# Gate products of 256 columns, issued through the helper of the large sums

## The chip, the cores and the metric

The kernel runs on one core of one Trainium2 chip. The metric is device time in microseconds of one launch. The profile comes from one execution and tells the span from the first to the last instruction; the device time of that execution is a little longer than its span.

## The reference, cut to what matters

One layer of a block with three parallel branches over 256 latent tokens and 256 context tokens of width 2048. The two places that the change touches are the recurrent gates (a block-diagonal product per head, two directions, two gates) and the pooling products (one 256 x 256 matrix per group):

```python
def _block_diag(u, w, b):                       # 8 heads of 128 channels
    y = jnp.einsum("blhi,hij->blhj", uh, w) + b
...
def _lru_coeffs(u, wr, br, wi, bi, lam):
    r = jax.nn.sigmoid(_block_diag(u, wr, br))
    i = jax.nn.sigmoid(_block_diag(u, wi, bi))
    log_a = -LRU_C * r * jax.nn.softplus(-lam)
    return jnp.exp(log_a), jnp.sqrt(-jnp.expm1(2.0 * log_a)) * i * u
...
def _multiscale_pool(u, n_rows, w_pool, s_pool):  # 4 groups of 256 channels
    ...                                           # p: window mean minus the token itself
    y = jnp.einsum("brngi,gij->brngj", p, w_pool)
    return y.reshape(bs, L, W_B) * s_pool
```

Around them stand an input projection of 2048 to 13312 columns, a depthwise convolution ahead of the recurrence and another of 31 taps, a layer norm, output projections of the branches, merge gates and a last projection.

## The kernel before, in words

Every fp32 product is made of three fp32r matmuls. Each operand is split into a high part (a cast by ScalarE) and a low part (a subtraction by VectorE), and high x high, high x low and low x high are summed in one PSUM bank.

**The large sums.** A weight piece of 128 x 2048 lands in `raws`, is split into `wh` and `wl` (line 84 and the helper at line 210), and is the stationary operand; the activations, `hH` and `hL`, 16 slots of 512 columns each, are the moving one. Most sums have 256 columns (the latent tokens) and 16 blocks of the contraction. The helper `columns` (lines 258 to 269) issues for each block high x high and high x low (lines 265, 266), and behind all of these the 16 low x high products (line 269): 48 matmuls of 256 columns.

**The short product.** `recent["pe"]` notes whether the last matmuls were wide (512 columns) or "columns" (256). Where a sum of 256 columns begins behind wide ones, `lead_in` (lines 250 to 256) issues one product of 64 columns first, on line 255; its result is overwritten by the sum. `wide` (line 245) issues one dummy product of 512 columns on line 247; one stands behind the pooling product, the layer norm's sums and the gate's sums.

**The recurrent gates.** Once the first projection is done (about 150 us), the context columns of `hH` and `hL` (256 to 512 of each slot) are free and serve as slots for smaller operands: the convolved input `u` of two heads in slots 8 to 11, the gate weights of one head in slots 14 and 15. `products(h, d)` (line 619) makes both gates of a head for one direction, over 512 tokens: per gate one bank of the small pool and three matmuls of 512 columns by `mm3` (lines 238 to 241). It is called 16 times. `gates` then reads the two banks with ScalarE (line 634 on).

**The pooling products.** `pool_end(g)` (line 846) is called once for each of the 4 groups. It makes two halves of a bank; each half sums two blocks of the contraction, by `mm3` on 256 columns. Its weights lie in slots 6 and 7, its input in slots 12 and 13. A wide dummy product follows.

**What sets the order.** The steps of the large sums are a fixed list. At each step the weights of the next one are split, work that has come due is issued (the pooling products among it), then the step's sum, and then as much background work as VectorE's estimated load leaves room for: the recurrence with its calls of `products` is such a chain. All 16 calls fall between large sums. Much later, at line 979, the output gate is summed with a matmul that waits for a chain of VectorE on weights which GpSimd's queue loads.

Of the kernel before, what the change touches and what calls it, by code (L numbers as in the profile page):

```python
# [145 lines left out]
def hybrid_block_kernel(  # L146
# [46 lines left out]
    def bank(pool=accp, tag="acc"):  # L193
        counter[0] += 1
        return pool.tile([P, 512], F32, tag=tag, name=f"{tag}{counter[0]}")

    def small_bank():
        return bank(smp, "sm")
# [9 lines left out]
    def tt(o, a, b, op):  # L208
        load["V"] += 0.09 + 0.00104 * size(o)
        V.tensor_tensor(out=o, in0=a, in1=b, op=op)  # L210
# [8 lines left out]
    def stt(o, a, s, b, op0, op1):  # L219
        load["V"] += 0.13 + 0.00104 * size(o)  # L220
        V.scalar_tensor_tensor(o, a, s, b, op0=op0, op1=op1)  # L221
# [5 lines left out]
    def scan(o, a, b, init):  # L227
        load["V"] += 0.13 + 0.00104 * size(o)
        V.tensor_tensor_scan(o, a, b, initial=init, op0=ALU.mult, op1=ALU.add)
# [4 lines left out]
    def split(H, Lo, src):  # L234
        A.copy(H, src)  # L235
        tt(Lo, src, H.bitcast(F32), ALU.subtract)

    def mm3(ps, sh, sl, mh, ml, start, stop):
        T.matmul(ps, sh, mh, start=start, stop=False)  # L239
        T.matmul(ps, sh, ml, start=False, stop=False)  # L240
        T.matmul(ps, sl, mh, start=False, stop=stop)  # L241

    recent = {"pe": "wide"}

    def wide(ps):

        T.matmul(ps, hH[:, 2, 0:128], hH[:, 0:2, 0:256], start=True, stop=True)
        recent["pe"] = "wide"

    def lead_in(job):  # L250


        ps, wh, _, mh, _ = job
        if recent["pe"] == "wide" and ps.shape[-1] == 256:
            T.matmul(ps[:, 0:64], wh[0], mh[0][:, 0:64], start=True, stop=True)
        recent["pe"] = "wide" if ps.shape[-1] == 512 else "columns"

    def columns(jobs):

        lead_in(jobs[0])
        for ps, wh, wl, mh, ml in jobs:
            for k in range(len(wh)):
                T.matmul(ps, wh[k], mh[k], start=k == 0, stop=False)  # L265
                T.matmul(ps, wh[k], ml[k], start=False, stop=False)  # L266
        for ps, wh, wl, mh, ml in jobs:
            for k in range(len(wh)):
                T.matmul(ps, wl[k], mh[k], start=False, stop=k == len(wh) - 1)  # L269
# [101 lines left out]
    with tc.manual_schedule():  # L371
# [82 lines left out]
        for n, (a, b) in enumerate(x_parts):  # L454
# [5 lines left out]
            for k in range(a, b):  # L460
                for j in range(4):
                    w = o + 512 * k + P * j
# [72 lines left out]
        def slots(i, n):  # L535
            return cH[:, i:i + n, :], cL[:, i:i + n, :]
# [4 lines left out]
        def take(name, lst):  # L541
            r = lst[rot[name] % len(lst)]
            rot[name] += 1
            return r
# [62 lines left out]
        def lru():  # L607
            la, lt, li = [ar[:, o:o + 2048].rearrange("p (h d l) -> p h d l", h=2, d=2) for o in (A_LA, A_LT, A_LI)]
            uH, uL = slots(8, 4)
            wH, wL = slots(14, 2)  # L610
            pss = {}

            def weights(h):
                raw = ws_t[0]
                split(wH, wL, raw.rearrange("p (a b) -> p a b", a=2))
                if h < 7:
                    nc.gpsimd.dma_start(raw, w_lru[h + 1])

            def products(h, d):
                i = h % 2  # L620
                for g in range(2):
                    ps = small_bank()
                    w = slice(128 * g, 128 * (g + 1))
                    mm3(ps.rearrange("p (s l) -> p s l", s=2), wH[:, d, w], wL[:, d, w],
                        uH[:, 2 * i:2 * i + 2, :], uL[:, 2 * i:2 * i + 2, :], True, True)
                    pss[g] = ps
                recent["pe"] = "wide"
                if d == 1:
                    lru_at["mm"] += 1

            def gates(h, d):
                i, c = h % 2, 8 * d + h
                ad, td, idd = la[:, i, d, :], lt[:, i, d, :], li[:, i, d, :]
                A.activation(ad, pss[0], AF.Tanh, scale=0.5, bias=brh[:, c:c + 1])
                A.activation(idd, pss[1], AF.Tanh, scale=0.5, bias=bih[:, c:c + 1])
                A.activation(td, ad, AF.Tanh, scale=tsp[:, c:c + 1], bias=tsp[:, c:c + 1])
                A.activation(ad, ad, AF.Exp, scale=nsp[:, c:c + 1], bias=nsp[:, c:c + 1])

            def gated(h, d):
                i = h % 2  # L640
                stt(li[:, i, d, :], li[:, i, d, :], 1.0, u_t[h % 4], ALU.add, ALU.mult)

            weights(0)
            ahead = False
            for pr in range(4):
                h0, h1 = 2 * pr, 2 * pr + 1
                if not ahead:
                    yield lambda: lru_at["split"] > pr
                    yield "S"
                    products(h0, 0)  # L650
                    yield "S"
                gates(h0, 0)
                products(h0, 1)
                yield "S"
                gates(h0, 1)
                weights(h1)
                gated(h0, 0)
                yield "S"
                products(h1, 0)
                gated(h0, 1)  # L660
                yield "S"
                gates(h1, 0)
                products(h1, 1)
                yield "S"
                gates(h1, 1)
                if pr < 3:
                    weights(h1 + 1)
                gated(h1, 0)
                yield "S"
                A.activation(lt, lt, AF.Sqrt, scale=0.25)  # L670
                gated(h1, 1)
                lru_at["u"] += 1
                yield "S"
                for i in range(2):
                    stt(lt[:, i], la[:, i], 1.0, lt[:, i], ALU.add, ALU.mult)
                    yield
                for i in range(2):
                    tt(lt[:, i], lt[:, i], li[:, i], ALU.mult)
                    yield
                ahead = pr < 3 and lru_at["split"] > pr + 1  # L680
                if ahead:
                    products(h1 + 1, 0)
                    yield "S"
                for i in range(2):
                    f, b = li[:, i, 0, :], li[:, i, 1, :]
                    scan(f[:, 256:512], la[:, i, 0, 256:512], lt[:, i, 0, 256:512], 0.0)
                    scan(b[:, ::-1], la[:, i, 1, ::-1], lt[:, i, 1, ::-1], 0.0)
                    yield
                    scan(f[:, 0:256], la[:, i, 0, 0:256], lt[:, i, 0, 0:256], f[:, 511:512])
                    yield  # L690
                for i in range(2):
                    tt(ya[:, h0 + i, :], li[:, i, 0, 0:256], li[:, i, 1, 0:256], ALU.add)
                    yield
# [148 lines left out]
        def put_p(k, t, src):  # L842
            H, Lo = slots(pslot[k] + t, 1)
            first.append((step_no[0] + 1, lambda: split(H[:, 0, :], Lo[:, 0, :], src)))

        def pool_end(g):
            bg.need(f"pool{g}")
            pH, pL = slots(12, 2)
            wH, wL = slots(6, 2)
            ps = bank()  # L850
            for j in range(2):
                for k in range(2):
                    mm3(ps[:, 256 * j:256 * (j + 1)], wH[:, k, 128 * j:128 * (j + 1)],
                        wL[:, k, 128 * j:128 * (j + 1)], pH[:, k, :], pL[:, k, :], k == 0, k == 1)
            wide(bank())
            for j in range(2):
                t = 2 * g + j
                pf = take("pf", pf_t)
                stt(pf, ps[:, 256 * j:256 * (j + 1)], vt[:, V_PS + t:V_PS + t + 1], zz_t[j], ALU.mult, ALU.mult)
                put_p(1, t, pf)  # L860
# [185 lines left out]
        for kind, key, item, q in steps:  # L1046
# [16 lines left out]
            if kind in ("xa", "xb", "zb", "cv", "cg", "za", "zc"):  # L1063
                ps = bank()
# [4 lines left out]
            elif kind == "gl":  # L1069
# [5 lines left out]
                ps = state["gl"][:, 256 * q:256 * (q + 1)]  # L1075
# [5 lines left out]
            elif kind == "bout":  # L1081
                k, j = key
                state["bout"] = bank()
                H, Lo = slots(pslot[k], 8)
                jobs = []
# [9 lines left out]
            elif kind == "out":  # L1095
                recent["gate"] = True
                if q == 0:
# [5 lines left out]
                    if key == 3:  # L1103
                        ps = bank()
# [37 lines left out]
            elif kind == "pwc":  # L1142
# [4 lines left out]
                jobs = []  # L1147
                for j in range(2):
                    ct = 2 * key + j
                    ps = bank()  # L1150
# [80 lines left out]
```

## Time and profile before

| | us |
|---|---|
| runs, not profiled | 971.37, 972.97, 977.41 (median 972.97) |
| profiled execution, device time | 973.01 |
| its span, first to last instruction | 971.2 |
| TensorE busy in it | 947.6 (98%) |
| VectorE, ScalarE, GpSimd busy in it | 738.9, 497.3, 40.8 |

In the profile PE is TensorE with its matmuls, PEld its weight loads, DVE VectorE, ACT ScalarE, POOL GpSimd; a `q` behind one of them means its queue of instructions. A matmul's duration includes the time in which the next one already streams, so the pace of TensorE is read from the start times of successive matmuls.

### The profile page before, as it was taken

The page shows a single profiled execution, that of the slowest core. Times are in us where ns is not written, and L with a number is a line of the kernel's source. Part 1 is how long each engine was busy: PE and PEld are TensorE (multiplying, and loading weights), DVE is VectorE, ACT ScalarE, POOL GpSimd, SP SyncE. Part 2 cuts the span into 40 slices and gives each one's busy share as a digit, 9 for nine tenths or more (in the row PEclk, how much of TensorE's full clock was granted, in tenths as well). Part 3 has the DMA queues.
Part 4 walks back from the last instruction along what each step waited for, and adds up shares of the span by engine and source line. Part 5 has one row for each costly group of instructions (what it writes and reads, how often), then busy time and mean ns, then how long its engine had stood idle before and what let it go on. Part 6 is the DMA issues. An engine that isn't in the chain of part 4 may idle for free.

```text
span 971.2 us, 18386 instructions
## 1 busy us (share of the span) xinstructions
PE 947.6 (98%) x7675; PEld 881.5 (91%) x7675; DVE 738.9 (76%) x1134; ACT 497.3 (51%) x657; POOL 40.8 (4%) x74
## 2 busy tenths in 40 slices
PE   6899999999999999999999999999999999999996
PEld 3576679999999999999999999999999899998885
DVE  3445457867875876899999999996665887898864
ACT  3223336567666677674444534344674444444442
POOL 0000010000100000000000000000002011101000
PEclk9999999999999999999999999999999999999999
DMA  9799955555545554555555555555459788878542
GB/s 371 300 420 379 358 195 191 185 192 177 189 145 192 174 204 161 174 178 197 194 206 182 196 195 197 194 191 200 173 197 361 243 313 327 306 262 309 202 169 88
DMA packets 34724, 220.72 MB, mean 227 GB/s; under 512 B 4128, under 2 KB 4272, under 8 KB 11856
## 3 DMA queue, kind: packets, MB, share of 16 engines
q1 hardware_dynamic: 28080, 195.28, 55.6%
q0 software_dynamic: 6560, 24.26, 7.4%
q8 instruction: 60, 0.98, 0.4%
q14 instruction: 24, 0.20, 0.1%
HBM read 217.43 MB, written 2.10 MB: 226 GB/s over the span
## 4 chain that ended last, share of the span: by engine, by line
PE 95%; DMA 2%; DVE 1%; ACT 1%; issue 1%; SPq 0%; ACTq 0%; DVEq 0%
PE acc L265 24%; PE acc L266 24%; PE acc L269 24%; PE acc L504 7%; PE sm L409 3%; PE acc L1117 3%; PE acc L1119 3%; PE acc L1120 3%; DMA raws<-in_w_ada_dram 2%; PE sm L504 1%; PE sm L240 1%; PE sm L239 1%; PE sm L241 1%; ACT hH L433 0%; DVE ar L210 0%
## 5 line engine op out<-in xcount | busy, mean ns | idle before, releaser
L265 PE MATMUL acc<-hH,wh 128*128 128x256 f32 (+1 forms) x2000 | 466.8, 278 | 0.0
L266 PE MATMUL acc<-hL,wh 128*128 128x256 f32 (+1 forms) x2000 | 464.6, 277 | 0.0
L84 ACT CAST wh<-raws 128x1024 fp32r<-128x1024 f32 (+1 forms) x288 | 298.4, 1052 | 259.4 <-PE acc L266 220.1
L210 DVE TENSOR_TENSOR wl<-raws,wh 128x1024 fp32r<-128x1024 f32 (+1 forms) x288 | 339.4, 1217 | 107.3 <-ACT wh L84 53.7
L265 PEld LDWEIGHTS acc<-hH,wh 128*128 128x128 f32 x2000 | 375.6, 188 | 1.7
L266 PEld LDWEIGHTS acc<-hL,wh 128*128 128x128 f32 x2000 | 375.8, 188 | 0.7
L269 PE MATMUL acc<-hH,wl 128*128 128x256 f32 (+1 forms) x2000 | 253.4, 277 | 0.0
L269 PEld LDWEIGHTS acc<-hH,wl 128*128 128x128 f32 x2000 | 239.4, 188 | 0.7
L221 DVE SCALAR_TENSOR_TENSOR ar<-ar,vt 128x256 f32<-128x256 f32 (+1 forms) x264 | 115.3, 503 | 0.0
L210 DVE TENSOR_TENSOR ar<-ar 128x512 f32<-128x512 f32 (+8 forms) x126 | 79.5, 654 | 8.4 <-DMA ar<-in_xt_dram 7.0
L221 DVE SCALAR_TENSOR_TENSOR ar<-ar,sc 128x512 f32<-128x512 f32 x64 | 48.0, 751 | 18.3 <-DMA ar<-in_w_gate_dram 16.9
L1119 PE MATMUL acc<-wh,hH 128*128 128x512 f32 (+1 forms) x144 | 51.8, 369 | 0.0
L1120 PE MATMUL acc<-wh,hL 128*128 128x512 f32 (+1 forms) x144 | 51.3, 366 | 0.0
L210 DVE TENSOR_TENSOR hL<-ar,hH 128x256 fp32r<-128x256 f32 (+1 forms) x76 | 39.5, 548 | 12.3 <-ACT hH L235 11.7
L215 DVE TENSOR_SCALAR sml<-sm,vt 128x2 f32<-128x2 f32 x16 | 3.5, 219 | 45.0 <-PE sm L417 45.0
L504 PE MATMUL acc<-hH,wh 128*128 128x512 f32 x96 | 29.3, 415 | 4.7 <-ACT hH L433 3.4
L433 ACT ACTIVATE hH<-ar,sml 128x256 fp32r<-128x256 f32 x32 | 17.5, 595 | 31.0 <-DVE sml L215 31.0
L411 ACT COPY ar<-sm 128x256 f32<-128x256 f32 x16 | 6.0, 374 | 51.5 <-PE sm L409 51.5
L1117 PE MATMUL acc<-wl,hH 128*128 128x512 f32 (+1 forms) x144 | 32.1, 366 | 0.0
L1120 PEld LDWEIGHTS acc<-wh,hL 128*128 128x128 f32 x144 | 27.0, 188 | 4.8 <-issue 0.2
L1119 PEld LDWEIGHTS acc<-wh,hH 128*128 128x128 f32 x144 | 27.0, 188 | 4.8 <-issue 0.2
L221 DVE SCALAR_TENSOR_TENSOR ar<-ar,acc 128x256 f32<-128x256 f32 (+1 forms) x56 | 29.6, 529 | 0.7 <-ACT ar L918 0.4
(145 smaller groups left out, 697.5 us busy)
## 6 DMA issues: line engine op xcount, KB each, us to landing
raws<-in_w_br_dram SPq DMA_DIRECT2D x49, 1024.0 KB, 4.9
raws<-in_w_gl_dram SPq DMA_DIRECT2D x48, 1024.0 KB, 4.9
raws<-in_w_bout_dram SPq DMA_DIRECT2D x24, 1024.0 KB, 4.9
raws<-in_w_ada_dram SPq DMA_DIRECT2D x16, 1024.0 KB, 9.9
ar<-in_w_ada_dram SPq DMA_DIRECT2D x16, 1024.0 KB, 9.9
ar<-in_w_gate_dram POOLq DMA_DIRECT2D x32, 512.0 KB, 5.9
raws<-in_w_out_dram SPq DMA_DIRECT2D x16, 1024.0 KB, 4.9
ar<-in_w_xa_dram SPq DMA_DIRECT2D x5, 896.0 KB, 11.5
```

Of the source, the lines that this page charges most:

```text
L84: self.nc.scalar.copy(h[:, 0:w], src)
L210: V.tensor_tensor(out=o, in0=a, in1=b, op=op)
L221: V.scalar_tensor_tensor(o, a, s, b, op0=op0, op1=op1)
L265: T.matmul(ps, wh[k], mh[k], start=k == 0, stop=False)
L266: T.matmul(ps, wh[k], ml[k], start=False, stop=False)
L269: T.matmul(ps, wl[k], mh[k], start=False, stop=k == len(wh) - 1)
L409: T.matmul(ps[32 * j:32 * j + 32, :], sc[:, k, :], raw[:, q, :], start=k < 4, stop=k >= 12)
L433: A.activation(hH[:, kt, w], h[:, w], AF.Identity, scale=gg[:, s:s + 1], bias=sh[:, s:s + 1])
L504: T.matmul(xa_ps[t], (wh, wh, wl)[a][:, P * t:P * (t + 1)], (hH, hL, hH)[a][:, kt, :], start=kt == 0 and a == 0, stop=kt == KT - 1 and a == 2)
L1117: T.matmul(ps, H, wl[:, w], start=False, stop=kt == KT - 1)
L1119: T.matmul(ps, H, wh[:, w], start=kt == 0, stop=False)
L1120: T.matmul(ps, Lo, wh[:, w], start=False, stop=False)
```

## The change

`products` issues each gate as two halves of 256 columns (latent and context tokens), each half as one call of `columns` with a single block; `recent["pe"]` is then "columns" and no longer "wide". `pool_end` issues each half of its bank by `columns` with two blocks. `mm3` is not called any more.

```diff
             def products(h, d):
                 i = h % 2
+                jobs = []
                 for g in range(2):
                     ps = small_bank()
                     w = slice(128 * g, 128 * (g + 1))
-                    mm3(ps.rearrange("p (s l) -> p s l", s=2), wH[:, d, w], wL[:, d, w],
-                        uH[:, 2 * i:2 * i + 2, :], uL[:, 2 * i:2 * i + 2, :], True, True)
+                    jobs += [(ps[:, 256 * s:256 * (s + 1)], [wH[:, d, w]], [wL[:, d, w]], [uH[:, 2 * i + s, :]],
+                              [uL[:, 2 * i + s, :]]) for s in range(2)]
                     pss[g] = ps
-                recent["pe"] = "wide"
+                for job in jobs:
+                    columns([job])
...
             for j in range(2):
-                for k in range(2):
-                    mm3(ps[:, 256 * j:256 * (j + 1)], wH[:, k, 128 * j:128 * (j + 1)],
-                        wL[:, k, 128 * j:128 * (j + 1)], pH[:, k, :], pL[:, k, :], k == 0, k == 1)
+                columns([(ps[:, 256 * j:256 * (j + 1)], [wH[:, k, 128 * j:128 * (j + 1)] for k in range(2)],
+                          [wL[:, k, 128 * j:128 * (j + 1)] for k in range(2)], [pH[:, k, :] for k in range(2)],
+                          [pL[:, k, :] for k in range(2)])])
             wide(bank())
```

## Rows read from the trace of the kernel before

**Rows 1.** The page: span, engines, and the chain that ended last.

```profile
span 971.2 us, 18386 instructions
...
PE 947.6 (98%) x7675; PEld 881.5 (91%) x7675; DVE 738.9 (76%) x1134; ACT 497.3 (51%) x657; POOL 40.8 (4%) x74
...
PE 95%; DMA 2%; DVE 1%; ACT 1%; issue 1%; SPq 0%; ACTq 0%; DVEq 0%
```

**Rows 2.** Waits of TensorE: for whom, us in total, times, longest.

```profile
PE acc L446 <- DMA ar<-in_xt_dram: 6.9, 1, 6.9
...
PE acc L979 <- issue: 1.8, 1, 1.8
```

**Rows 3.** Groups of matmuls by line and shape: count, busy us, mean ns, idle before.

```profile
L265 PE MATMUL acc<-hH,wh 128*128 128x256 f32 x1984 | 460.4, 277 | 0.0
...
L239 PE MATMUL sm<-hH 128*128 128x512 f32 x32 | 12.6, 395 | 0.0
...
L255 PE MATMUL acc<-hH,wh 128*128 128x64 f32 x24 | 4.6, 192 | 0.0
...
L239 PE MATMUL acc<-hH 128*128 128x256 f32 x16 | 4.5, 282 | 0.0
```

**Rows 4.** TensorE in order of time, one recurrent product: start, us, line.

```profile
302.66 1.98 PE L269 MATMUL acc<-hH,wl 128*128 128x256 f32 x16
304.47 0.40 PE L239 MATMUL sm<-hH 128*128 128x512 f32 x1
...
305.86 0.19 PE L255 MATMUL acc<-hH,wh 128*128 128x64 f32 x1
305.89 0.36 PE L265 MATMUL acc<-hH,wh 128*128 128x256 f32 x1
306.09 0.28 PE L266 MATMUL acc<-hL,wh 128*128 128x256 f32 x1
...
306.32 0.28 PE L266 MATMUL acc<-hL,wh 128*128 128x256 f32 x1
```

**Rows 5.** The same view, one pooling product and the sum behind it.

```profile
185.10 0.28 PE L239 MATMUL acc<-hH 128*128 128x256 f32 x1
...
186.54 0.39 PE L247 MATMUL acc<-hH 128*128 128x512 f32 x1
...
187.00 0.28 PE L266 MATMUL acc<-hL,wh 128*128 128x256 f32 x1
...
187.59 0.28 PE L265 MATMUL acc<-hH,wh 128*128 128x256 f32 x1
```

**Rows 6.** The same view, a recurrent product with a pooling product right behind it.

```profile
210.17 0.40 PE L239 MATMUL sm<-hH 128*128 128x512 f32 x1
...
211.56 0.28 PE L239 MATMUL acc<-hH 128*128 128x256 f32 x1
...
212.99 0.39 PE L247 MATMUL acc<-hH 128*128 128x512 f32 x1
```

**Rows 7.** GpSimd in order of time, start of the output gate's loads.

```profile
728.57 0.73 POOL L963 DMA_DIRECT2D ar<-in_xs_dram  x1 [356.27 <-DVE hL L210]
```

**Rows 8.** The chain in order of time: start, us, 16 matmuls each.

```profile
683.17 1.81 PE acc L269 x16
...
774.44 1.88 PE acc L269 x16
...
820.74 1.81 PE acc L269 x16
```

**Rows 9.** Stretches of TensorE: us, busy (count), granted clock, DMA share, GB/s.

```profile
422.81:662.25 239.44, 239.44 (x2114) 1.00 0.56 194
770.42:815.73 45.31, 45.31 (x386) 1.00 0.84 309
816.86:855.02 38.16, 38.16 (x338) 1.00 0.83 296
```

**Rows 10.** Groups by line and shape, from 281.12 to 662.25 us alone.

```profile
L265 PE MATMUL acc<-hH,wh 128*128 128x256 f32 x1072 | 248.1, 277 | 0.0
```

## The prediction

> **What bounds the kernel now.** I read the page first. TensorE is busy for 98% of a 971.2 us span, and the chain of work that ended last runs through it for 95% [rows 1]. Then I read what TensorE waited for: 6.9 us for the first transfers, long before the change's place, and 1.8 us ahead of line 979, long after it [rows 2]. The groups of the recurrent products, of the pooling products and of the large sums around them have no idle time before them at all [rows 3]. So where the edit lies only one thing counts: the time from one matmul's start to the next. The durations that the profile gives for matmuls (276 to 395 ns) overlap and say nothing of this; start times do.
>
> Three paces can be read. The large sums, which alternate products of 256 columns, take 302.66 to 304.47 us for 16 matmuls, 113 ns each [rows 4]. The recurrent products of 512 columns take 304.47 to 305.86 us for six, 232 ns each or 116 ns per 256 columns [rows 4]. The pooling products, already of 256 columns, take 185.10 to 186.54 us for twelve, 120 ns each [rows 5].
>
> **What the recurrent products cost now.** Each of the 16 calls (32 matmuls of line 239, two per call [rows 3]) issues six matmuls of 512 columns, and the next large sum then begins with the short product of line 255. In the example, 304.47 to 306.32 us holds the six, the short one and three matmuls of the next sum: 1.85 us. Three matmuls at the settled 113 ns are 0.34, so a call costs 1.51 us: about 1.39 for the six, 0.03 for the short one, 0.09 because the first matmul behind it is followed only after 0.20 us and the pace needs one more to settle [rows 4].
>
> **What they cost afterwards.** Twelve matmuls of 256 columns each, with no short product behind them, since the helper now notes "columns". Nothing in the trace is this exact operation, so I bound its pace. From below: 113 ns as in the large sums, 12 x 0.1133 = 1.36 us. From above: 120 ns as in the pooling products, 1.44 us. I take 120, because the pooling product is the nearer row in both respects in which it differs from a large sum. First, its stationary and its moving operand both lie in hH and hL, as those of the recurrent gates do (slots 14 and 8 against slots 6 and 12), whereas the large sums take the stationary one from wh or wl. Second, with only one block of the contraction the "order of the large sums" is high-high, high-low, low-high for each half: exactly the order in which the pooling products run now at 120 ns. The reordering that the change speaks of exists only where there are two blocks, in the pooling. Whichever of the two makes the 120 ns, the recurrent products have it.
>
> The Trainium skill says, on its page Perfetto Trace Analysis, section Optimizing Tensor Performance (Matmuls), that larger matmuls are more efficient than smaller ones where possible. Here 116 ns per 256 columns inside a 512 against 120 agrees with it and 113 speaks against it, so the rule holds only by the operands [rows 4, 5]; by the rule the twelve would cost at least the present 1.39 us.
>
> The return to the large sum has no row either. At best it costs nothing; at worst 0.09 as now. Nearest is the settling behind a pooling product once the short product has passed: 187.00 to 187.59 us for five matmuls, 0.02 over the settled pace [rows 5]. So a call costs 1.44 + 0.02 = 1.46 instead of 1.51, a gain of 0.05 us.
>
> **Where a pooling product follows.** Of the 16 calls, two are followed at once by a pooling product, with no short product between. In the first, 210.17 to 212.99 us is 2.82 us now [rows 6]; 24 matmuls at 120 ns would be 2.88, a loss of 0.06 each. The other two pooling products take 1.44 us and would keep that if the location of the operands sets their pace; if the order does, each of the four gains 12 x 6.7 ns = 0.08 us. I take no gain. The wide product behind each pooling product and its short product stay.
>
> **Nothing else moves.** The change issues no transfer and touches no other queue; what ScalarE reads (the two banks of a call) is complete some hundredths of a microsecond later or earlier, and ScalarE is busy for only 51% of the span [rows 1]. The gain must still pass the wait ahead of line 979 [rows 2], which is set by VectorE and the gate's transfers. It does: that chain starts on GpSimd only when a split of VectorE ends at 728.57 us [rows 7], and those splits are paced by TensorE, so the whole chain comes earlier by what was gained. If it did not, the wait would eat the gain and the result would be no change.
>
> **Sum.** 14 x 0.05 = 0.7 gained (0.66 unrounded), 2 x 0.06 = 0.12 lost: 0.5 us faster. The profiled execution took 973.01 us (span 971.2 and 1.8 around it), and the median of the three runs, 972.97, is the same within 0.1. Forecast 973.01 - 0.5 = 972.5 us. The runs of before spread from 971.4 to 977.4, so nothing under about 1% (9.7 us) is told from no change by a measurement of this kernel.
>
> **Rivals.**
> 1. Everything runs at 113 ns. Then 14 x (1.51 - 1.36) = 2.1, 2 x (2.82 - 2.72) = 0.2 and 2 x 0.08 = 0.16: 2.5 us, 970.6. For it: the large sums hold this pace whatever slot of hH and hL they read, and they are most of the kernel [rows 3]. Against it: the pooling products run at 120 ns behind a large sum and behind a recurrent product alike (211.56 to 212.99 us for twelve) [rows 5, 6]. The Trainium skill, on the page TensorE: Matmul & The Clock Gate, section Part 2: What happens when you issue a matmul, gives TensorE two independent read ports and says that loading the next weights takes nothing from the running matmul. By that rule the place of the operands could not matter and this rival would come out; the pooling rows, at 120 ns, speak against it [rows 5].
> 2. Only the pooling gains (order sets the pace, and the recurrent products keep theirs): 0.5 + 4 x 0.08 = 0.8, 972.2 us.
> 3. The large sums behind the products get stuck at a slow pace. This is the way to a slower kernel. The trace has it: around 774 us the same large sums take 1.88 us for 16 matmuls instead of 1.81 [rows 8], and the whole stretch from 770 to 816 us, up to the next wide product, stays so: 45.31 us for 386 matmuls, 117 ns, at a granted clock of 1.00 [rows 9]. Price 0.07/16 = 4.4 ns a matmul. That state came of how one sum was entered; the short product, which usually lets the pace settle within five matmuls [rows 4, 5], is what the change takes away behind the recurrent products. From 281 to 662 us there is no wide product left that could end the state, and three groups of 1072 matmuls each run there [rows 10]: 3216 x 4.4 ns = 14 us, so 972.5 + 14 = 986.5 us, 1.4% slower. If only the last call leaves it, the 2114 matmuls behind that call up to 662 us make 9 us [rows 9]. What decides is the offset at which the first weight load of a sum follows a product at 120 ns. Against it: the sums behind the pooling products came back from that very pace, though over a wide and a short product [rows 5], and two entries behind other wide products have settled where the rows at 683 and 821 us stand [rows 8].
> 4. The change does not do what it says: the noted state keeps the short products. The helper sets "columns" for a width of 256, so I give this nothing beyond the sum's own uncertainty; 14 x 0.03 us hang on it.
>
> **Chances.** Forecast 0.60, rival 1 0.19, rival 2 0.08, rival 3 0.13 (0.09 of it beyond 1%, the rest when only some returns stick). The predicted time is the likeliest case. The range holds the forecast and rivals 1 and 2, 970.6 to 972.5, and, on both sides, what the three entries behind line 979 can do by chance: the stuck stretch of 770 to 816 us may settle this time (386 x 4.4 ns = 1.7 us less), the next one of 338 matmuls may stick (1.5 us more) [rows 9], and some tenths to a microsecond from run to run. That gives 969.3 to 975.3 and leaves out the 0.13 of rival 3. Faster by over 1% has no mechanism: all calls together cost 16 x 1.51 = 24 us, of which 22 remain even at 113 ns; 0.02 for the unknown. Slower by over 1%: 0.09. Within: 0.89.
>
> **What the profile afterwards will show.** Lines 239 to 241 are gone; lines 265, 266 and 269 appear on the small banks, 64 times each; line 255 falls from 24 to 10. If I am right, the twelve matmuls of a call are 120 ns apart, and the next sum is at 113 ns within about five. Starts 113 ns apart in the products mean rival 1; 113 in the pooling alone, rival 2. Large sums of 16 matmuls in 1.88 us between 281 and 662 us mean rival 3, and then the prediction is wrong. It would be wrong in size as well if the wait ahead of line 979 grew by what came before it.

## The result and the profile after

The changed kernel takes 984.63 us (median; 983.05 to 987.47) against 973.10 before, a ratio of 1.0122 with a 95% interval of 1.0098 to 1.0146. It is slower by 1.2%. Forecast were 972.5 us with a range up to 975.3; what came has the place and nearly the size of rival 3, which had been priced at 986.5 us and given 0.13.

The page of the changed kernel, its span and engines:

```profile
span 983.6 us, 18550 instructions
...
PE 961.4 (98%) x7757; PEld 898.6 (91%) x7757; DVE 739.4 (75%) x1134; ACT 497.2 (51%) x657; POOL 40.8 (4%) x74
```

The span grew by 12.4 us and TensorE's busy time by 13.8 (947.6 in [rows 1]); no other engine's busy time moved by more than 0.5 us. Next the groups of matmuls by line and shape (count, busy us, mean ns, idle before), which answer to [rows 3]:

```profile
L265 PE MATMUL sm<-hH 128*128 128x256 f32 x64 | 18.1, 283 | 0.0
...
L255 PE MATMUL acc<-hH,wh 128*128 128x64 f32 x10 | 1.9, 192 | 0.0
```

The change did what it says: 64 products on the small banks per line, 10 short products instead of 24, still no idle time. Then TensorE in order of time, one recurrent product and the sum behind it, against [rows 4], and one pooling product, against [rows 5]:

```profile
185.86 0.28 PE L265 MATMUL acc<-hH 128*128 128x256 f32 x1
...
187.30 0.39 PE L247 MATMUL acc<-hH 128*128 128x512 f32 x1
...
306.37 0.28 PE L265 MATMUL sm<-hH 128*128 128x256 f32 x1
306.49 0.28 PE L266 MATMUL sm<-hL,hH 128*128 128x256 f32 x1
...
307.69 0.28 PE L269 MATMUL sm<-hH,hL 128*128 128x256 f32 x1
307.80 0.28 PE L265 MATMUL acc<-hH,wh 128*128 128x256 f32 x1
307.92 0.28 PE L266 MATMUL acc<-hL,wh 128*128 128x256 f32 x1
308.04 0.28 PE L265 MATMUL acc<-hH,wh 128*128 128x256 f32 x1
308.16 0.28 PE L266 MATMUL acc<-hL,wh 128*128 128x256 f32 x1
```

A call takes 306.37 to 307.80, 1.43 to 1.44 us, 120 ns a matmul, as forecast. A pooling product takes 1.44 us, as before; its new order changed nothing. But the sum behind the call goes on at 0.12 us a matmul, and it does not settle. The chain in order of time shows how far that reaches (start, us for 16 matmuls; compare [rows 8]):

```profile
202.34 1.81 PE acc L269 x16
209.36 1.89 PE acc L269 x16
218.12 1.81 PE acc L269 x16
...
675.20 1.89 PE acc L269 x16
686.96 1.81 PE acc L269 x16
```

Ahead of the first call the sums are fast, behind it slow, behind a pooling product fast again, and behind the last call slow up to the layer norm's wide product near 677 us. The stretches of TensorE alone (us, busy and count, granted clock, DMA share, GB/s), against [rows 9]:

```profile
428.18:676.93 248.75, 248.75 (x2115) 1.00 0.53 187
784.45:828.05 43.60, 43.60 (x386) 1.00 0.83 305
```

The 2112 matmuls behind the last call take 248.75 us instead of 239.44, 4.4 ns more each, with the granted clock at 1.00 both times. With the stretches behind the other calls, 3 x 1072 matmuls from 281 us on [rows 10] and 96 earlier ones, 3312 x 4.4 ns = 14.6 us are lost. The calls themselves give back 14 x 0.07 and lose 2 x 0.06 = 0.9 net; the stretch that was stuck before (770 to 816 us, 45.31 us) happens to settle this time, 43.60 us, 1.7 back; the wait ahead of the gate's matmul is 0.6 shorter; the start came 0.8 later (the first pooling product begins at 185.86 instead of 185.10). 14.6 - 0.9 - 1.7 - 0.6 + 0.8 = 12.2 of the 12.4.

### The profile page after: what moved, and what is told of

The parts are those of the page before. It is cut to its first block, busy times and chain, and to the rows that moved or that the text cites. A ratio compares the mean times of both kernels' runs of the same rounds, so it can differ in the third digit from the quotient of the medians.

```text
span 983.6 us, 18550 instructions
## 1 busy us (share of the span) xinstructions
PE 961.4 (98%) x7757; PEld 898.6 (91%) x7757; DVE 739.4 (75%) x1134; ACT 497.2 (51%) x657; POOL 40.8 (4%) x74
## 4 chain that ended last, share of the span: by engine, by line
PE 96%; DVE 1%; ACT 1%; DMA 1%; issue 0%; ACTq 0%; SPq 0%; DVEq 0%
PE acc L265 24%; PE acc L266 24%; PE acc L269 24%; PE acc L504 7%; PE sm L409 3%; PE acc L1119 3%; PE acc L1121 3%; PE acc L1122 3%; PE sm L504 1%; PE sm L266 1%; PE sm L265 1%; PE sm L269 1%; PE acc L446 1%; DMA ar<-in_xt_dram 1%; PE acc L463 1%
## 5 line engine op out<-in xcount | busy, mean ns | idle before, releaser
L265 PE MATMUL acc<-hH,wh 128*128 128x256 f32 (+1 forms) x2000 | 473.9, 280 | 0.0
L266 PE MATMUL acc<-hL,wh 128*128 128x256 f32 (+1 forms) x2000 | 472.9, 280 | 0.0
L269 PE MATMUL acc<-hH,wl 128*128 128x256 f32 (+1 forms) x2000 | 257.8, 280 | 0.0
L269 PEld LDWEIGHTS acc<-hH,wl 128*128 128x128 f32 x2000 | 243.4, 188 | 0.7
```

## The experiments

Two things lay open: what lets a sum settle at 113 ns or stick at 118, and what makes twelve matmuls run at 120. Ten kernels were run; "before" is the kernel before, run on the same chip in the same session. e2, e4 and e6 to e9 were run once; for them the stretches of the trace carry the reading, and not the time. A summary stands ahead; each row is the pace of the large sums behind the calls, in ns a matmul.

| ahead of the sum | weights of the gates in | short product | sum behind | kernel |
|---|---|---|---|---|
| six of 512 columns | slots | yes | 113 | before |
| six of 512 | slots | no | 118 | e2 |
| six of 512 | tensors of their own | no | 118 | e7 |
| twelve of 256 | slots | no | 118 | the change |
| twelve of 256 | slots | yes | 118 | e1 |
| twelve of 256 and a wide one | slots | yes | 113 | e9 |
| twelve of 256 | slots, high and low swapped | no | 118 | e3 |
| twelve of 256 | tensors of their own behind hL | no | 113 | e4, e5 |
| twelve of 256 | tensors of their own ahead of all | no | 113 | e6 |
| twelve of 256 | high in slots, low apart | no | 113 | e8, odd heads |
| twelve of 256 | high apart, low in slots | no | 118 | e8, even heads |

**e1: the short product put back behind the new calls.**

```diff
                 for job in jobs:
                     columns([job])
+                recent["pe"] = "wide"
```

> The changed kernel with one thing undone: after each recurrent product the note is wide again, so that the short product of 64 columns stands ahead of the next large sum. Theory A (the lost short product let the large sums stick at 118 ns): the twelve matmuls of a call stay 120 ns apart, the sums behind settle at 113 ns within about five matmuls, and the 3312 slow matmuls give back 4.4 ns each, 14.7 us: 970 us in the state of the later stretches that the changed kernel shows, 972 if the stretch of 384 sticks again. Theory B (the products of 256 columns themselves throw TensorE into the slow pace, whatever follows): the sums stay at 118 ns and the time stays near 984.6 us.

Measured: 986.39 us against 971.05, ratio 1.0169 (1.0143 to 1.0195). Theory A is wrong as it stood. TensorE in order of time, the end of a call, the short product and the sum, and below it the stretch behind the last call:

```profile
306.19 0.28 PE L269 MATMUL sm<-hH,hL 128*128 128x256 f32 x1
306.30 0.19 PE L255 MATMUL acc<-hH,wh 128*128 128x64 f32 x1
306.33 0.36 PE L265 MATMUL acc<-hH,wh 128*128 128x256 f32 x1
306.53 0.28 PE L266 MATMUL acc<-hL,wh 128*128 128x256 f32 x1
306.65 0.28 PE L265 MATMUL acc<-hH,wh 128*128 128x256 f32 x1
```

```profile
427.67:676.45 248.78, 248.78 (x2115) 1.00 0.52 187
```

The short product stands there and costs its 0.03 and the gap of 0.20 behind it, as in [rows 4], but the sum sticks: 248.78 us. Theory B holds for these products: their loss is not the lost short product.

**e2: the kernel before without its short product.**

```diff
                     pss[g] = ps
-                recent["pe"] = "wide"
```

> The kernel before with one line taken out: the recurrent products stay 512 columns wide, but no short product follows. Theory A1 (any block that is not followed by a short product lets the next sum stick): large sums at 118 ns between 204 and 662 us, about 14 us slower than before, 987 us. Theory A2 (only products at 120 ns leave the offset that sticks, 512 columns do not): sums at 113 ns, 14 x 0.12 = 1.7 us faster than before or nearly so, 971 to 973 us.

Measured: 983.91 us (one time; before 971.05). The stretch behind the last call:

```profile
425.35:674.05 248.70, 248.70 (x2113) 1.00 0.53 186
```

Behind products of 512 columns the short product is what lets the sums settle (theory A1). So there are two ways into the slow pace, and one cure that works for only one of them.

**e3: high and low gate weights swapped between hH and hL**, in the changed kernel.

```diff
-            wH, wL = slots(14, 2)
+            wL, wH = slots(14, 2)
```

> The changed kernel with the high part of the gate weights stored in hL and the low part in hH: while a matmul streams from one of the two tensors, the next weights load from the other in every pair. Theory C (120 ns comes of stationary and moving operand lying in the same tensor): the twelve matmuls of a call are 113 ns apart, the sums behind stay at 113 ns without a short product, and the time is 14 x 0.15 + 0.2 = 2.3 us below the kernel before, about 970 us. Theory D (it does not matter in which of the two tensors an operand lies): 120 ns, sums at 118 ns, 984.6 us as the changed kernel.

Measured: 984.06 us against 971.05, ratio 1.0138 (1.0121 to 1.0156). TensorE in order of time, the first and last matmul of a call and the sum's first; then the stretch behind the last call:

```profile
307.58 0.28 PE L265 MATMUL sm<-hH,hL 128*128 128x256 f32 x1
...
308.90 0.28 PE L269 MATMUL sm<-hH 128*128 128x256 f32 x1
309.02 0.28 PE L265 MATMUL acc<-hH,wh 128*128 128x256 f32 x1
```

```profile
429.39:678.10 248.71, 248.71 (x2114) 1.00 0.52 186
```

Still 1.44 us a call, and the sums stick. The swap sees to it that the next weights always load from the tensor that is not being streamed just then, so a load from the streamed tensor is not the cause (theory C falls in that form). That the weights lie in one of the two at all stays possible.

**e4: the weights of the second direction in two small tensors of their own**, laid out behind hL; two small constants moved into an unused part of the large work tensor to make room.

```diff
+    apart = [cst.tile([P, 256], F32R, name=f"apart{i}") for i in range(2)]
...
+                    gH, gL = (apart[0][:, w], apart[1][:, w]) if d == 1 else (wH[:, 0, w], wL[:, 0, w])
-                    jobs += [(ps[:, 256 * s:256 * (s + 1)], [wH[:, d, w]], [wL[:, d, w]], [uH[:, 2 * i + s, :]],
+                    jobs += [(ps[:, 256 * s:256 * (s + 1)], [gH], [gL], [uH[:, 2 * i + s, :]],
```

> The changed kernel with the gate weights of the second direction in two small tensors of their own, neither in hH nor in hL; those of the first direction stay. Theory C (the place of the operands sets the pace): calls of the second direction run at 113 ns, those of the first at 120; the sums behind the second (2784 of the 3312 slow matmuls) return to 113 ns, which gives back 12.4 us: about 972 us. Theory D (the place does not matter; 120 ns comes of the order high-high, high-low, low-high or of something else): all calls at 120 ns, all sums behind them at 118 ns, 984.6 us.

Measured: 970.66 us (one time; before 971.05). The stretches behind a call of the first direction, of a call of the second, behind it, and behind the last call:

```profile
281.34:292.65 11.31, 11.31 (x98) 1.00 0.43 148
292.65:294.05 1.40, 1.40 (x14) 1.00 0.75 316
294.06:304.93 10.87, 10.87 (x98) 1.00 0.54 182
424.06:663.40 239.34, 239.34 (x2114) 1.00 0.54 194
```

In one kernel 96 matmuls of the same kind take 11.31 us behind weights from the slots and 10.87 behind weights from elsewhere, with neither a wide nor a short product between; in the change the sums behind both directions stick. The place of the weights decides about the sum (theory C in its wider form). The call itself does not run at 113, as theory C had it: it was entered at 118 and keeps that (1.41 us), and only the sum behind it returns. The weight loads of the low products show the place too (line 270, both directions; count, duration in ns: least, median, most):

```profile
L270 PEld LDWEIGHTS sm<-hH,hL x32: 192/192/192, 203.2 to 416.8; 128*128 128x128 f32 x32
L270 PEld LDWEIGHTS sm<-hH,apart x32: 187/188/188, 210.3 to 423.8; 128*128 128x128 f32 x32
```

The longer load is a sign and not the whole cause: in e8, below, low weights from `apart` load in 192 ns as well, and the sum behind them returns. The Trainium skill, TensorE: Matmul & The Clock Gate, section Part 2: What happens when you issue a matmul, says that loading weights takes no read bandwidth from the running matmul, having a read port of its own. Here the calls run at 120 ns with the weights in the slots (the change) and at 113 with the weights apart (e5, below), so by the measurement the place of the weights matters; whether read bandwidth is what it costs, no run shows.

**e5: the weights of both directions in those two tensors**, split for one direction at a time, just ahead of use.

```diff
-            def weights(h):
+            def weights(h, d):
                 raw = ws_t[0]
-                split(wH, wL, raw.rearrange("p (a b) -> p a b", a=2))
+                split(apart[0], apart[1], raw[:, 256 * d:256 * (d + 1)])
...
+                weights(h0, 1)
                 gates(h0, 0)
                 products(h0, 1)
```

> The changed kernel with the gate weights of both directions in the two small tensors, split for one direction at a time; none lie in the slots of hH and hL any more, and no short product follows. Theory E (weights loaded from the slots bring the 120 ns and push the next sum into 118; weights from elsewhere leave the pace as it was): calls and sums behind them at 113 ns, 14 x 0.15 + 0.2 = 2.3 us below the kernel before of the same session, about 969 us. Theory F (a call leaves the other pace than the one it was entered at, since in the earlier run calls entered at 118 were left at 113): sums behind every second call stick at 118, some 5 to 10 us slower.

Measured: 968.05 us against 971.86, ratio 0.9960 (0.9940 to 0.9981): faster than the kernel before by 0.4%, and the only one here that is shown to be. TensorE in order of time, a call and the sum behind it; then the stretch behind the last call:

```profile
299.84 0.28 PE L266 MATMUL sm<-hH,apart 128*128 128x256 f32 x1
299.95 0.28 PE L267 MATMUL sm<-hL,apart 128*128 128x256 f32 x1
...
301.08 0.28 PE L270 MATMUL sm<-hH,apart 128*128 128x256 f32 x1
301.20 0.28 PE L266 MATMUL acc<-hH,wh 128*128 128x256 f32 x1
301.31 0.28 PE L267 MATMUL acc<-hL,wh 128*128 128x256 f32 x1
301.42 0.28 PE L266 MATMUL acc<-hH,wh 128*128 128x256 f32 x1
```

```profile
417.42:656.75 239.33, 239.33 (x2114) 1.00 0.55 194
```

A call takes 1.36 us, 113 ns a matmul, and the sum goes on at 113 without a break. That is rival 1's state for the calls, reached by moving the weights; theory F is out. The price of 2.3 us lies within the measured interval (1.8 to 5.8 us), but so does the 1.7 us that the stretch behind the gate's matmul can give or take, and in the profiled execution that stretch settled; the times alone do not tell the two apart. One call met its low weights late, with TensorE idle for 0.3 us on VectorE's split; the matmuls behind that wait ran at 118, and the sum settled all the same.

**e6: as e4, with the two tensors laid out ahead of all others.**

```diff
+    apart = [cst.tile([P, 256], F32R, name=f"apart{i}") for i in range(2)]
     ar = cst.tile([P, A_N], F32, name="ar")
```

> The same as the run with the weights of the second direction apart, but the two small tensors are laid out ahead of all others instead of behind hL, so that their addresses lie below hH and not above hL. Theory G (it is the region of the address that counts, above or below the operand that streams): calls of the second direction at 120 ns and sums stuck behind them, about 984 us. Theory H (only the slots of hH and hL are bad): as in the run with the tensors behind hL, sums behind the second direction at 113 ns, about 971 us.

Measured: 973.23 us (one time; before 971.86). A call, the sum behind it and the stretch behind the last call:

```profile
294.31:295.73 1.42, 1.42 (x14) 1.00 0.74 312
295.74:306.62 10.88, 10.88 (x98) 1.00 0.52 179
425.87:665.20 239.33, 239.33 (x2114) 1.00 0.55 193
```

Sums behind the second direction settle (theory H). The call takes 1.43 us instead of 1.41, so the address plays some part within it; which, stays open.

**e7: products of 512 columns without the short product, weights of the second direction apart.**

```diff
+                    gH, gL = (apart[0][:, w], apart[1][:, w]) if d == 1 else (wH[:, 0, w], wL[:, 0, w])
-                    mm3(ps.rearrange("p (s l) -> p s l", s=2), wH[:, d, w], wL[:, d, w],
+                    mm3(ps.rearrange("p (s l) -> p s l", s=2), gH, gL,
...
-                recent["pe"] = "wide"
```

> Products of 512 columns without the short product, with the weights of the second direction apart. Theory E: sums behind calls of the second direction go back to 113 ns even though no short product follows, those behind the first direction stick at 118; about 971 us. Theory I (behind a product of 512 columns only the short product helps, wherever the weights lie): all sums behind calls at 118 ns, 984 us.

Measured: 981.94 us (one time; before 971.86). Behind the last call, one of the second direction:

```profile
425.13:673.85 248.72, 248.72 (x2113) 1.00 0.53 186
```

Stuck (theory I). Behind 512 columns the place of the weights does not help, so the two ways into the slow pace do not share this cure either.

**e8: for the second direction only the high weights apart (even heads), or only the low ones (odd heads).**

```diff
...
+                    if d == 1:
+                        gH, gL = (apart[0][:, w], gL) if h % 2 == 0 else (gH, apart[1][:, w])
```

> The changed kernel with, for the second direction, only the high weights apart (even heads) or only the low weights apart (odd heads). Theory J (the weights of the last matmul of a call decide how the next sum runs; it is a low one): sums behind odd heads at 113 ns, behind even heads at 118; the last call is odd, so 2112 + 192 x 3 matmuls or so are fast: about 973 us. Theory K (any weights from the slots within the call suffice): all sums stuck, 984 us.

Measured: 974.12 us (one time; before 971.86). The sum behind an even head, the sum behind an odd one, and the stretch behind the last call, an odd head:

```profile
295.58:306.88 11.30, 11.30 (x98) 1.00 0.55 189
...
315.39:337.14 21.75, 21.75 (x194) 1.00 0.47 158
426.85:666.20 239.35, 239.35 (x2114) 1.00 0.55 193
```

96 matmuls in 11.30 us are slow, 192 in 21.75 fast. So the low weights, which the call's four low products and with them its last matmul use, decide about the sum, not those of the eight high ones (theory J). The last matmul alone was not separated from the other three low ones.

**e9: a wide dummy product behind each new call**, which brings the short one with it.

```diff
                 for job in jobs:
                     columns([job])
+                wide(bank())
```

> The changed kernel with a wide dummy product behind each call of the recurrent products, so that a wide and a short product stand ahead of the next large sum, as they do behind the pooling products. Theory L (the pair of a wide and a short product settles the sums, each alone does not): calls at 120 ns, sums behind them at 113 ns; 16 x (0.23 + 0.03 + 0.1) us are paid for the pair, 14.7 us given back: about 975 us. Theory M (the pair helps only behind the pooling products): sums at 118 ns, 990 us.

Measured: 976.55 us (one time; before 972.12). The sum behind the second call, and the stretch behind the last:

```profile
296.35:307.33 10.98, 10.98 (x98) 1.00 0.55 194
428.65:668.10 239.45, 239.45 (x2114) 1.00 0.54 193
```

The 96 matmuls take 10.98 us with the short product's gap in them, the 2112 take 239.45: at 113 ns (theory L). The wide and the short product together settle what the short one alone (e1) does not; the wide one alone was not run. The pair costs more than the calls won.

Yet the pair is no sure cure. The stretch of the kernel before that stuck at 770 us [rows 9] stands behind such a pair, the wide and the short product behind the gate's matmul:

```profile
769.76 0.80 PE L247 MATMUL sm<-hH 128*128 128x512 f32 x1
770.40 0.19 PE L255 MATMUL acc<-hH,wh 128*128 128x64 f32 x1
```

In e2 the sum at the same place stuck as well:

```profile
781.28:826.58 45.30, 45.30 (x386) 1.00 0.84 300
```

In the traces of the change, of e1 and of e3 to e9 it settled, behind the same instructions. What tells these entries apart was not found.

**e10: the change of the pooling products alone**, in the kernel before.

> The kernel before with the change of the pooling products alone. The pooling products of the changed kernel already run 1.44 us for twelve, as before, so no change by more than 0.1 us; a theory by which the order of the pooling products costs or gains something would show twelve at other than 1.43 to 1.44 us.

Measured: 972.14 us against 972.12, ratio 1.0004 (0.9993 to 1.0015). That part of the change is worth nothing either way. The edit does one thing more than the text of the change says: two of the four pooling products follow a recurrent product directly, and where the note is still "wide" there, `columns` issues a short product ahead of them. Their twelve matmuls then take 1.52 us instead of 1.43 (210.61 to 212.13 us); the other two take 1.44, as before. So it is the short product, and not the order, that costs there, about 0.2 us in all. The same short product stands in e1 and e9; in the change it does not.

## Why the prediction was wrong

**Right.** TensorE's pace alone decides in this stretch. The calls run at 120 ns and the pooling products, in their new order, too, so order does not set that pace and rival 2 is out. The wait ahead of the gate's matmul follows TensorE, as the prediction had it: TensorE came there 14 us later, and the wait was 1.2 us instead of 1.8. Of the two grounds for taking 120, the place of the operands is the real one, at least that of the weights: with the weights out of hH and hL the same calls run at 113 (e5).

**The step that failed** is "The return to the large sum". Its term was bounded by 0 and 0.09 us a call, and 0.02 was taken. Measured, the return does not come at all: the sums keep 118 ns, which costs 0.44 us for 96 matmuls (11.31 against 10.87 us, e4), 9.3 us for the 2112 behind the last call, and 14.6 us in all. The 0.02 was read off the settling behind a pooling product, "once the short product has passed". That row stands behind a wide and a short product, and the changed kernel has neither behind its calls. With both put there the sums return (e9), with the short one alone they do not (e1), and with the low weights elsewhere they return without either (e4, e8). So what was missing from the sum is the state in which products with low weights from the slots leave TensorE.

**Rival 3 came out, but not by the way it gave.** Its place and price were right (14 us; 14.6 measured), and its chance of 0.13 was too low. It held that the short product is what lets the pace settle; behind 512 columns that is so (e2), behind 256 with weights from the slots it is not (e1). That the offset of a sum's first weight load decides, as it says, no run shows. And as evidence against it stood that sums came back from "that very pace" behind the pooling products, "though over a wide and a short product": the half-sentence was the whole matter. Evidence that holds only through what the change removes is none. Without it, nothing in the trace spoke for a return, and the stuck stretch [rows 8, 9] spoke against it the more, since it sticks even behind a wide and a short product (e9). Two figures of the prediction are a little off: that stretch holds 384 matmuls (the 386 count one of each neighbour), so its pace is 118 ns and not 117; and the range's lower end by its own terms is 970.6 - 1.7 = 968.9 us, not 969.3.

**The rule on size.** The Trainium skill, Perfetto Trace Analysis, section Optimizing Tensor Performance (Matmuls), calls larger matmuls more efficient than smaller ones, when possible. For the call itself it depends on the weights' place: 1.36 us (e5) and 1.44 (the change) as twelve, 1.39 as six [rows 4], with the weights apart too (e7). Nothing in it covers the sums behind, where the time went.

**Open.** Why weights loaded from those slots slow a matmul of 256 columns, why the two sets of tensors apart do so less or not at all, why a wide and a short product together end the slow pace, and why they twice did not at 770 and 781 us, is not settled. That the streaming operand would matter likewise was not tried; there is no room to move it.

## What to carry to other kernels

Where matmuls follow one another without idle time, read the distance between starts in the stretches behind an edit, not only in the edited instructions: 24 us of products were changed here, and 14.6 us were lost in sums that nobody touched. A row that shows a recovery counts only if what brought the recovery about is still there after the change. Here products of 256 columns among long sums did no harm once their weights, at least the low ones that the last product uses, lay in a small tensor of their own; elsewhere that is worth a try, with a look at the first ten matmuls behind them.

## What the runs showed of the hardware

Matmuls of 256 columns ran at three paces with the granted clock at 1.00: 113 ns, 118 ns (248.75 us for 2112) and 120 ns (the calls of the change, the pooling products). The 118 is kept by sums that, entered differently, hold 113 for as long. It was entered from six products of 512 columns unless a short product followed (e2, e7); from products of 256 columns whose low weights come from the slots, short product or not (e1, the change); within a call behind a wait of 0.3 us (e5); and twice behind a wide and a short product (the kernel before at 770 us, e2 at 781). It was left through a wide and a short product (the change at 677 us), or through products whose low weights lie elsewhere (e4, e6, e8).
